# Turning a head pair's keys behind the next pair's scores in an RWKV-7 stage on one Trainium2 core

## The chip, the core and the metric

The program runs on one core of a Trainium2 chip. The core has five engines that each work through a queue of their own in order: TensorE (PE, with its weight loads shown apart as PEld), VectorE (DVE), ScalarE (ACT), GpSimd (POOL) and SyncE (SP, which only issues DMAs here). An engine waits for another through semaphores. The metric is the device time of one execution in microseconds, and the kernel before is given as the median of 3 runs. Beside it stands one profiled execution, from which every duration and every start below is taken. L12 is line 12 of the kernel before, except where the changed kernel is named.

## The reference

The trunk takes x of 1 x 512 x 1024 in float32. It has two layers, each a token mixer and a gated feed-forward block with a causal convolution, and a final RMSNorm. The mixer of the first layer is a chunked spatial gating MLP, that of the second the RWKV-7 time mixing, which the change touches:

```
r, k, v = xr @ w_r, xk @ w_k, xv @ w_v                     # xr, xk, ...: token-shifted mixes
w = -softplus(-(w0 + tanh(xw @ w1) @ w2)) - 0.5
a = sigmoid(a0 + (xa @ a1) @ a2);  g = sigmoid(xg @ g1) @ g2
kk = k * k_k, scaled to length 1 in each of 16 heads of 64
k = k * (1 + (a - 1) * k_a);  decay = exp(-exp(w))
for t in range(512):                                       # state S: 64 x 64 per head
    S = S * decay[t] + (S @ -kk[t]) (kk[t] * a[t])^T + v[t] k[t]^T
    y[t] = S @ r[t]
y = group_norm(y) * ln_w + ln_b + sum(r * k * r_k) * v
out = (y * g) @ w_o
```

The loop over tokens is computed in 8 chunks of 64 tokens. Within a chunk the products of keys and receptances form 64 x 64 triangular matrices (the scores), one of which must be inverted per head and chunk. From chunk to chunk only the state is handed on, by a product with "turned" keys: keys transposed and multiplied with the decay of the whole chunk.

## The kernel before

**Arithmetic.** A dense product in float32 is made of three matmuls on numbers split in a high and a low part (L320, L321, L322). Each has 128 rows and columns of the array and 512 columns of output. Other products are single matmuls on parts of the array: 64 rows x 128 columns for scores and turned keys, 64 x 64 in the scan, 32 x 32 in the inversion.

**Stages.** SGU mixer, feed-forward, RWKV-7 mixer, feed-forward, final norm. The mixer of RWKV-7 stands between about 573 and 850 us of the span. In it three streams of work are woven together by `weave`: a main one, a side one and a fill.

**The pairs (main).** Heads are worked through in 8 pairs p, one head on rows 0 to 63 of the array and one on rows 64 to 127. `pairs()` runs through them. For pair p it starts the decay steps of pair p + 2 (`decay`, matmuls L863, L865, L887, L895 into the "e" banks), makes the operands of pair p + 1 (`operands`: tiles ar and bk, two buffers each), and makes the products of pair p (`products`). These are:

- dg (L931, DVE): diagonal matrices of the chunk decays.
- Two halves of the scores, 4 chunks each. Each half is 16 matmuls (L938) of bk with ar, 8 for each head, one head into an "aux" bank and the other into a "us" bank. DVE evicts both with the masks into lq (L942), ACT copies a part into ti, the input of the inversion (L943), and three DMAs on SP's queue store lq into the DRAM scratch std (L946).
- Turned keys: 16 matmuls of bk with dg (L952), again 8 per head into "aux" and "us". ACT copies them into bt (L955) and SP stores bt into the DRAM scratch btd (L956).

A step of the decay of pair p + 2 follows each of the three. `done.add(p)` then marks the pair. `done` is what the stages below and the centering of values (`value`, L832, L838, and the bonus L847) go by.

**The inversion (side).** `invert(g)` inverts the triangles of four pairs at once: g = 0 for pairs 0 to 3, g = 1 for pairs 4 to 7. It copies ti, or a part of it, into a block tile (L1003 on DVE for g = 1), transposes it (L1006), runs 31 steps of two DVE instructions (L1014, L1015), transposes back (L1020 and the line behind it), and joins the blocks with two products of 32 x 32 matmuls (L1033, then L1036) through "aux" banks.

**The scan.** `scan(g)` goes through the 8 chunks of four pairs: products with the state (L1207, L1211), DVE's copy wt (L1210), the product with the inverse (L1220), the product with the turned keys that makes the next state (L1229), and the output (L1234). `load(g, c)` brings a chunk's operands back from DRAM on SP's queue: scores st (L1150), values vu (L1156), turned keys cbt (L1157). Chunk 0 of g = 0 is loaded earlier and into other tiles.

**The fill** is dense work: key and value projections, gates, and the output projection.

**What sets the order.** The stages are weaves one behind the other: the pairs until pair 3 is in `done`; then with inversion 0 beside them until pair 6 is; then `load(0, 0)`; then the rest of the pairs; then the pool of the pairs is closed and the pool of the scan takes its memory; then the scan of g = 0 with inversion 1 beside it; then the scan of g = 1. `weave` advances the side and the fill by rates per step of the main stream. `issue_after(x)` holds an instruction behind x on its engine. Within these bounds a scheduling layer fixes the order of each engine's queue when the program is built. PSUM is shared out by four tags, "mm", "aux", "e" and "us", with two banks each.

## Time and profile before

| | |
|---|---|
| median of 3 runs | 1267.81 us (1267.59 to 1269.96) |
| the profiled execution, its own time | 1264.91 us |
| its span, first to last instruction | 1263.1 us |
| mean granted clock of TensorE | 0.997 |
| PE, DVE, ACT busy in 600 to 640 us | 40.00, 32.11, 28.46 |
| in 720 to 760 us | 39.23, 37.35, 23.08 |
| in 760 to 800 us | 37.19, 29.25, 27.47 |
| in 800 to 850 us | 45.85, 35.88, 18.79 |

A row of the timeline gives start, duration, engine, line, operation, output and inputs, the rows and columns of the array for a matmul, shapes and a count. In square brackets stands how long the engine had been idle before it, and what ended that. Matmuls are pipelined, so their durations overlap, and what one costs is read from start to start. Rows of windows give a stretch of the span, its length, and each engine's busy time in it with the count of its instructions, then the granted clock, the share of DMA time and the rate in GB/s.

### The profile page before, as it was taken

The page shows a single profiled execution, that of the slowest core. Times are in us where ns is not written, and L with a number is a line of the kernel's source. Part 1 is how long each engine was busy: PE and PEld are TensorE (multiplying, and loading weights), DVE is VectorE, ACT ScalarE, POOL GpSimd, SP SyncE. Part 2 cuts the span into 40 slices and gives each one's busy share as a digit, 9 for nine tenths or more (in the row PEclk, how much of TensorE's full clock was granted, in tenths as well). Part 3 has the DMA queues.
Part 4 walks back from the last instruction along what each step waited for, and adds up shares of the span by engine and source line. Part 5 has one row for each costly group of instructions (what it writes and reads, how often), then busy time and mean ns, then how long its engine had stood idle before and what let it go on. Part 6 is the DMA issues. An engine that isn't in the chain of part 4 may idle for free.

```text
span 1263.1 us, 19531 instructions
## 1 busy us (share of the span) xinstructions
PE 1241.9 (98%) x7591; PEld 1007.9 (80%) x7591; DVE 856.1 (68%) x1403; ACT 629.7 (50%) x1082; POOL 98.0 (8%) x121
## 2 busy tenths in 40 slices
PE   9999999999999999999999999899999999999997
PEld 6878888888888888877777776678888888888886
DVE  6466568888886454675789897765677777773233
ACT  6544446556555433475676657423544544443322
POOL 4100200000000010000000022222000000000002
PEclk9999999999999999999999999999999999999998
DMA  7332357777656765325868799764222333333332
GB/s 258 104 100 84 130 167 240 247 252 245 195 166 203 228 215 184 97 91 192 218 200 226 215 244 230 213 171 138 96 95 91 99 100 100 96 88 105 92 92 80
DMA packets 115452, 201.65 MB, mean 160 GB/s; under 512 B 21600, under 2 KB 53600, under 8 KB 115360
## 3 DMA queue, kind: packets, MB, share of 16 engines
q10 hardware_dynamic: 39104, 112.87, 29.3%
q1 hardware_dynamic: 76256, 87.54, 23.2%
q8 instruction: 59, 0.97, 0.3%
q14 instruction: 33, 0.27, 0.1%
HBM read 152.93 MB, written 47.45 MB: 159 GB/s over the span
## 4 chain that ended last, share of the span: by engine, by line
PE 86%; DVE 6%; DMA 1%; issue 1%; ACT 1%; POOL 0%; SPq 0%; DVEq 0%; ACTq 0%; POOLq 0%
PE mm L320 9%; PE mm L322 9%; PE mm L321 9%; PE aux L320 6%; PE aux L322 6%; PE aux L321 6%; PE e L321 6%; PE e L320 6%; PE e L322 6%; PE us L321 5%; PE us L322 5%; PE us L320 5%; PE aux L938 1%; DVE tt L1015 1%; DVE pr L1014 1%; PE aux L952 1%
## 5 line engine op out<-in xcount | busy, mean ns | idle before, releaser
L236 ACT CAST w<-w 128x512 fp32r<-128x512 f32 x340 | 206.5, 611 | 360.8 <-PE e L322 91.1
L237 DVE TENSOR_TENSOR w<-w,w 128x512 fp32r<-128x512 f32 x340 | 232.1, 685 | 184.7 <-ACT w L236 184.4
L320 PE MATMUL mm<-mxh,w 128*128 128x512 f32 x416 | 169.7, 408 | 0.2 <-ACT vt L837 0.2
L321 PE MATMUL mm<-mxl,w 128*128 128x512 f32 x416 | 163.8, 394 | 0.0
L322 PE MATMUL mm<-mxh,w 128*128 128x512 f32 x416 | 163.7, 394 | 0.0
L347 POOL TENSOR_TENSOR ss<-ss,sq 128x512 f32<-128x512 f32 x30 | 40.7, 1355 | 770.7 <-issue 592.9
L320 PEld LDWEIGHTS mm<-mxh,w 128*128 128x128 f32 x416 | 78.1, 188 | 20.1 <-issue 3.3
L322 PEld LDWEIGHTS mm<-mxh,w 128*128 128x128 f32 x416 | 78.2, 188 | 16.7 <-issue 0.7
L321 PEld LDWEIGHTS mm<-mxl,w 128*128 128x128 f32 x416 | 78.2, 188 | 15.5 <-issue 1.3
L545 ACT ACTIVATE cv<-z,par 128x512 f32<-128x512 f32 x88 | 71.7, 817 | 29.4 <-DVE z L543 24.4
L322 PE MATMUL aux<-mxh,w 128*128 128x512 f32 x216 | 84.2, 390 | 0.3 <-DVE w L237 0.3
L320 PE MATMUL aux<-mxh,w 128*128 128x512 f32 x216 | 84.5, 391 | 0.0
L320 PE MATMUL us<-mxh,w 128*128 128x512 f32 x216 | 84.5, 391 | 0.0
L321 PE MATMUL aux<-mxl,w 128*128 128x512 f32 x216 | 84.1, 389 | 0.0
L321 PE MATMUL us<-mxl,w 128*128 128x512 f32 x216 | 84.1, 389 | 0.0
L322 PE MATMUL us<-mxh,w 128*128 128x512 f32 x216 | 84.0, 389 | 0.0
L320 PE MATMUL e<-mxh,w 128*128 128x512 f32 x208 | 81.4, 391 | 0.1
L321 PE MATMUL e<-mxl,w 128*128 128x512 f32 x208 | 81.1, 390 | 0.1
L322 PE MATMUL e<-mxh,w 128*128 128x512 f32 x208 | 80.9, 389 | 0.0
L546 DVE SCALAR_TENSOR_TENSOR cv<-z,par,cv 128x512 f32<-128x512 f32 x88 | 66.1, 752 | 19.9 <-ACT cv L545 19.9
L547 DVE SCALAR_TENSOR_TENSOR cv<-z,par,cv 128x512 f32<-128x512 f32 x88 | 66.0, 752 | 2.9
L322 PEld LDWEIGHTS aux<-mxh,w 128*128 128x128 f32 x216 | 40.5, 188 | 9.2 <-DVE w L237 0.8
(1089 smaller groups left out, 2574.8 us busy)
## 6 DMA issues: line engine op xcount, KB each, us to landing
w<-in_wup ACTq DMA_DIRECT2D x88, 512.0 KB, 3.6
w<-in_wdn ACTq DMA_DIRECT2D x32, 512.0 KB, 3.7
st<-std SPq DMA_DIRECT2D x30, 320.0 KB, 6.2
w<-wkd ACTq DMA_DIRECT2D x16, 512.0 KB, 4.9
w<-wvd ACTq DMA_DIRECT2D x16, 512.0 KB, 5.6
w<-wod ACTq DMA_DIRECT2D x16, 512.0 KB, 4.2
w<-in_wdn ACTq DMA_DIRECT2D x16, 384.0 KB, 3.4
w<-in_wsu ACTq DMA_DIRECT2D x8, 512.0 KB, 3.7
```

Of the source, the lines that this page charges most:

```text
L236: nc.scalar.copy(hi[r, :n], src)
L237: (lo_eng or nc.vector).tensor_tensor(lo[r, :n], src, hi[r, :n].bitcast(F32), ALU.subtract)
L320: mm(acc, wh, xh, start=first, stop=False)
L321: mm(acc, wh, xl, start=False, stop=False)
L322: mm(acc, wl, xh, start=False, stop=last)
L347: nc.gpsimd.tensor_tensor(self.ss, self.ss, self.sq, ALU.add)
L545: nc.scalar.activation(c, z[:, 2:], AF.Identity, scale=cw(2, i), bias=self.p("conv_b", l * 44 + i))
L546: nc.vector.scalar_tensor_tensor(c, z[:, 1:T + 1], cw(1, i), c, ALU.mult, ALU.add)
L547: nc.vector.scalar_tensor_tensor(c, z[:, 0:T], cw(0, i), c, ALU.mult, ALU.add)
L938: nc.tensor.matmul(qs[hd][:, c - ch.start, :], bk[H[hd], c, C * hd:C * hd + P], ar[H[hd], c, :], start=True, stop=True)
L952: nc.tensor.matmul(qs[hd][:, c, :], bk[H[hd], c, C * hd:C * hd + P], dg[H[hd], c, :], start=True, stop=True)
L1014: V.tensor_tensor(q, a, b, ALU.mult)
```

## The change

`products` is split in three. `scores(p, u, half)` makes one half of the scores; its first matmul is returned as `lead`, and the 15 others are held behind it. `diagonals(p, u)` makes dg. `turned(p, u, lead)` makes the turned keys, all 16 matmuls held behind `lead`, and now does `done.add(p)`. In `pairs()`, the first half of pair p's scores is followed by the turned keys of pair p - 1, which used to stand behind the second half of their own pair; dg is made between the two halves; the turned keys of pair 7 come behind the loop. The context manager `behind` is new, and the scan's `batch` uses it in place of its own three lines. The instructions are the same in kind and number.

```diff
+        @contextmanager
+        def behind(lead):
+            with ExitStack() as stack:
+                if lead is not None:
+                    stack.enter_context(tc.issue_after(lead))
+                yield
...
-        def products(p, u):
+        def scores(p, u, half):
...
-            dg = tile_([P, NCH, C], "dg", 1)
-            V.tensor_tensor(dg, self.c("id2", C).unsqueeze(1).to_broadcast([P, NCH, C]), bc(gc[:, p], C), ALU.mult)
             masks = self.c("masks", P)
-
-            for ch in (slice(0, U), slice(U, NCH)):
-                qs = [self.acc(tag).rearrange("p (c t) -> p c t", t=P) for tag in ("aux", "us")]
-                for c in range(ch.start, ch.stop):
-                    for hd in range(2):
+            ch = slice(U * half, U * half + U)
+            qs = [self.acc(tag).rearrange("p (c t) -> p c t", t=P) for tag in ("aux", "us")]
+            lead = None
+            for c in range(ch.start, ch.stop):
+                for hd in range(2):
+                    with behind(lead):
                         nc.tensor.matmul(qs[hd][:, c - ch.start, :], bk[H[hd], c, C * hd:C * hd + P], ar[H[hd], c, :],
                                          start=True, stop=True)
...
+                    lead = lead or self.last(mybir.EngineType.PE)
...
+            return lead
+
+        def diagonals(p, u):
+
+            u.dg = tile_([P, NCH, C], "dg", 1)
+            V.tensor_tensor(u.dg, self.c("id2", C).unsqueeze(1).to_broadcast([P, NCH, C]), bc(gc[:, p], C), ALU.mult)
+
+        def turned(p, u, lead=None):
+
             bt = tile_([P, NCH, 2, C], "bt", BT)
             qs = [self.acc(tag).rearrange("p (c t) -> p c t", t=C) for tag in ("aux", "us")]
-            for c in range(NCH):
-                for hd in range(2):
-                    nc.tensor.matmul(qs[hd][:, c, :], bk[H[hd], c, C * hd:C * hd + P], dg[H[hd], c, :],
-                                     start=True, stop=True)
+            with behind(lead):
+                for c in range(NCH):
+                    for hd in range(2):
+                        nc.tensor.matmul(qs[hd][:, c, :], u.bk[H[hd], c, C * hd:C * hd + P], u.dg[H[hd], c, :],
+                                         start=True, stop=True)
             for hd in range(2):
                 S.copy(bt[:, :, hd, :], qs[hd])
             nc.sync.dma_start(btd[:, :, p].rearrange("c p a t -> p c (a t)"), bt.rearrange("p c a t -> p c (a t)"))
-            yield
+            done.add(p)
...
-                for _ in products(p, units[p]):
-                    next(nxt, None)
-                    yield
-                done.add(p)
+                lead = scores(p, units[p], 0)
+                if p:
+                    turned(p - 1, units[p - 1], lead)
+                next(nxt, None)
+                yield
+                diagonals(p, units[p])
+                scores(p, units[p], 1)
+                next(nxt, None)
+                yield
+                next(nxt, None)
+                yield
+            turned(p, units[p])
+            yield
```

In the changed kernel the scores stand at L943, their evictions at L948 and L949, their stores at L952, dg at L958, the turned keys at L967 and their store at L971. The inversion's products are L1057 and L1060, the decay's matmuls L870, L872, L894 and L902, the bonus L854, the transposition L1030.

**First place: the last scores of pair 0 and the first of pair 1, on PE.** In the names, bk_4984 holds the keys of the earlier pair and bk_5090 those of the later one. Before, the turned keys stood by themselves between dense matmuls:

```order
L320 MATMUL mm_5072<-mxh_4838,w_794_5018 128x512
L321 MATMUL mm_5072<-mxl_4839,w_794_5018 128x512
L887 MATMUL e_5170<-cst,sq_5162 128x2 x4
L322 MATMUL mm_5072<-mxh_4838,w_794_5018 128x512
L952 MATMUL aux_5187<-dg_5098,bk_4984 128x64
L952 MATMUL us_5188<-dg_5098,bk_4984 128x64
...
L320 MATMUL mm_5217<-mxh_4759,w_803_5073 128x512
...
L322 MATMUL mm_5217<-mxh_4786,w_803_5073 128x512
L938 MATMUL aux_5251<-ar_5085,bk_5090 128x128
L938 MATMUL us_5252<-ar_5085,bk_5090 128x128
...
L863 MATMUL e_5269<-lr_4357,l_785_4998 128x512
```

In the changed kernel they follow the later pair's scores directly:

```order
L322 MATMUL mm_5195<-mxh_4786,w_803_5073 128x512
L943 MATMUL aux_5227<-ar_5085,bk_5090 128x128
L943 MATMUL us_5228<-ar_5085,bk_5090 128x128
...
L967 MATMUL aux_5246<-dg_5141,bk_4984 128x64
L967 MATMUL us_5247<-dg_5141,bk_4984 128x64
...
L870 MATMUL e_5267<-lr_4357,l_785_4998 128x512
L870 MATMUL e_5268<-lr_4358,l_786_4999 128x512
```

One stretch of 64-row matmuls stands where two were, and the turned keys have moved past a dozen dense matmuls.

**Second place: the start of the first inversion, on DVE.** In the names, sq_5808 and sq_5806 are decay tiles, li is the transposed block. Before:

```order
L942 TENSOR_TENSOR lq_5848<-us_5839,cst 128x4x128
L875 SCALAR_TENSOR_TENSOR sq_5808<-cst,sq_5808 128x512
L931 TENSOR_TENSOR dg_5971<-cst,gc 128x512
L1006 STREAM_TRANSPOSE li_5828<-ix_5827 128x32x32
L1014 TENSOR_TENSOR pr_5830<-li_5828,tt_5829 128x31
```

In the changed kernel:

```order
L948 TENSOR_TENSOR lq_5848<-aux_5838,cst 128x4x128
L948 TENSOR_TENSOR lq_5848<-us_5839,cst 128x4x128
L882 SCALAR_TENSOR_TENSOR sq_5806<-cst,sq_5806 128x512
L1030 STREAM_TRANSPOSE li_5826<-ix_5825 128x32x32
L948 TENSOR_TENSOR lq_5959<-aux_5949,cst 128x4x128
```

No dg stands ahead of the transposition any more, and the eviction of the next pair's first scores stands directly behind it.

**Third place: the end of the pairs, on PE.** Here bk_6171 (before) and bk_6149 (changed) hold the keys of pair 7, ix and li are the inversion's transposed blocks. Before:

```order
L1033 MATMUL aux_6310<-ix_6305,ti_4860 32x32 x16
L938 MATMUL aux_6360<-ar_6166,bk_6171 128x128 x4
L1033 MATMUL aux_6310<-ix_6305,ti_4860 32x32 x16
...
L938 MATMUL us_6453<-ar_6166,bk_6171 128x128 x3
L938 MATMUL aux_6452<-ar_6166,bk_6171 128x128 x4
...
L1036 MATMUL aux_6489<-li_6306,tt_6309 32x32 x16
L322 MATMUL mm_6508<-mxh_5501,w_1047_6331 128x512
...
L952 MATMUL us_6521<-dg_6358,bk_6171 128x64 x4
L952 MATMUL aux_6520<-dg_6358,bk_6171 128x64 x5
...
L1036 MATMUL aux_6489<-li_6306,tt_6309 32x32 x16
L832 MATMUL mm_6577<-cst,v_6506 128x128 x2
L1036 MATMUL aux_6559<-li_6306,tt_6309 32x32 x16
```

In the changed kernel:

```order
L1057 MATMUL aux_6395<-ix_6283,ti_4860 32x32 x16
L322 MATMUL mm_6508<-mxh_5537,w_1044_6309 128x512
L967 MATMUL us_6573<-dg_6450,bk_6149 128x64
L1060 MATMUL aux_6489<-li_6284,tt_6287 32x32 x32
L1060 MATMUL aux_6537<-li_6284,tt_6287 32x32 x16
L967 MATMUL us_6573<-dg_6450,bk_6149 128x64 x7
L1060 MATMUL aux_6537<-li_6284,tt_6287 32x32 x16
L320 MATMUL mm_6508<-mxh_5550,w_1045_6311 128x512
L321 MATMUL mm_6508<-mxl_5551,w_1045_6311 128x512
L967 MATMUL aux_6572<-dg_6450,bk_6149 128x64 x8
L322 MATMUL mm_6508<-mxh_5550,w_1045_6311 128x512
```

The turned keys of pair 7 stood ahead of three quarters of the inversion's second product (L1036); now half of them stand behind all of it (L1060), and the two heads' rows stand apart. On SP's queue the store of these keys is still the last of the pairs and still stands ahead of the loads of the scan's chunk 1.

More of the change, by code (lines that the diff above doesn't have):

```diff
@@ L2 @@
 import math
-from contextlib import ExitStack
+from contextlib import ExitStack, contextmanager
 import numpy as np
@@ L938, in products @@
                         nc.tensor.matmul(qs[hd][:, c - ch.start, :], bk[H[hd], c, C * hd:C * hd + P], ar[H[hd], c, :],
                                          start=True, stop=True)
-                lq = tile_([P, U, 2, P], "lq", 2)
-                for hd in range(2):
-                    V.tensor_tensor(lq[:, :, 1 - hd], qs[hd], masks.unsqueeze(1).to_broadcast([P, U, P]), ALU.mult)
-                    S.copy(ti[g][H[hd], i, ch], lq[H[hd], :, 1 - hd, 0:C])
-                f = lq.rearrange("p c a t -> p c (a t)")
@@ L945, in products @@
-                for hd, o, n, q in ((0, P, P, 0), (0, 2 * P, C, P + C), (1, 0, P + C, C)):
-                    nc.sync.dma_start(std[g][ch, H[hd], i, o:o + n].rearrange("c p t -> p c t"), f[H[hd], :, q:q + n])
-                yield
+                    lead = lead or self.last(mybir.EngineType.PE)
+            lq = tile_([P, U, 2, P], "lq", 2)
+            for hd in range(2):
+                V.tensor_tensor(lq[:, :, 1 - hd], qs[hd], masks.unsqueeze(1).to_broadcast([P, U, P]), ALU.mult)
+                S.copy(ti[g][H[hd], i, ch], lq[H[hd], :, 1 - hd, 0:C])
@@ new lines, in scores @@
+            f = lq.rearrange("p c a t -> p c (a t)")
+            for hd, o, n, q in ((0, P, P, 0), (0, 2 * P, C, P + C), (1, 0, P + C, C)):
+                nc.sync.dma_start(std[g][ch, H[hd], i, o:o + n].rearrange("c p t -> p c t"), f[H[hd], :, q:q + n])
+            return lead
[3 more added lines that the diff above has]
+        def turned(p, u, lead=None):
@@ L1178, in batch @@
                 for n, (i, hd) in enumerate(ih):
-                    with ExitStack() as behind:
-                        if lead is not None:
-                            behind.enter_context(tc.issue_after(lead))
+                    with behind(lead):
                         one(i, hd, n)
```

3 lines of the change are left out of this document (1 added, 2 removed).

## The prediction

> **What bounds the kernel now.** I read the page first, then the windows over the stage that the change touches, then the timelines of PE, DVE and SP there. Line numbers are those of the kernel before.
>
> ```profile
> span 1263.1 us, 19531 instructions
> PE 1241.9 (98%) x7591; PEld 1007.9 (80%) x7591; DVE 856.1 (68%) x1403; ACT 629.7 (50%) x1082; POOL 98.0 (8%) x121
> PE 86%; DVE 6%; DMA 1%; issue 1%; ACT 1%; POOL 0%; SPq 0%; DVEq 0%; ACTq 0%; POOLq 0%
> ```
>
> Over the whole span TensorE (PE) is the bound. The second row says 98% busy, and the third, the chain of waits, gives it 86%. But the average hides the stage in question. The windows (stretch, its length, then busy time and count of PE, PEld, DVE, ACT, POOL) show two bounds there:
>
> ```profile
> 640.00:680.00 40.00, 40.00 (x298) 30.05 (x297) 35.79 (x70) 30.59 (x57) 0.23 (x2) 1.00 0.76 216
> 680.00:700.00 20.00, 19.86 (x162) 16.23 (x162) 19.67 (x44) 11.83 (x25) 0.61 (x2) 1.00 0.79 231
> 730.00:740.00 10.00, 9.23 (x108) 7.03 (x108) 9.52 (x23) 5.17 (x10) 1.64 (x3) 1.00 1.02 273
> 740.00:750.00 10.00, 10.00 (x135) 7.10 (x133) 9.60 (x21) 5.96 (x14) 2.56 (x6) 1.00 1.08 270
> 750.00:760.00 10.00, 10.00 (x128) 8.08 (x128) 9.56 (x28) 4.13 (x10) 3.27 (x3) 1.00 1.06 238
> 780.00:790.00 10.00, 7.99 (x186) 6.25 (x186) 5.00 (x11) 6.91 (x13) 4.39 (x6) 1.00 0.81 209
> ```
>
> Up to 680 PE has no idle time and VectorE (DVE) has some, so PE time saved there is time saved. From 680 to 700, and from 730 to 760, DVE is as full as PE, because it carries the two inversions (L1014, L1015). There, PE time saved may only become waiting. From 780 to 790 PE stands idle for 2.0 us.
>
> **What a change of array shape costs.** This is the price that the change is about: a batch of 64-row matmuls between dense ones (PE timeline: start, duration, line, rows*columns of the array).
>
> ```profile
> 602.58 0.39 PE L321 MATMUL mm<-mxl,w 128*128 128x512 f32 x1
> 602.81 0.39 PE L322 MATMUL mm<-mxh,w 128*128 128x512 f32 x1
> 603.13 0.37 PE L938 MATMUL aux<-ar,bk 64*128 64x128 f32 x1
> 603.14 0.37 PE L938 MATMUL us<-ar,bk 64*128 64x128 f32 x1
> 603.34 0.27 PE L938 MATMUL aux<-ar,bk 64*128 64x128 f32 x1
> ...
> 603.46 0.27 PE L938 MATMUL aux<-ar,bk 64*128 64x128 f32 x1
> ...
> 604.01 0.27 PE L938 MATMUL aux<-ar,bk 64*128 64x128 f32 x1
> ...
> 604.22 0.50 PE L320 MATMUL mm<-mxh,w 128*128 128x512 f32 x1
> 604.56 0.39 PE L321 MATMUL mm<-mxl,w 128*128 128x512 f32 x1
> ...
> 712.95 1.16 PE L938 MATMUL aux<-ar,bk 64*128 64x128 f32 x8
> 714.03 0.69 PE L1033 MATMUL aux<-ix,ti 32*32 32x32 f32 x32
> ```
>
> From start to start, dense matmuls take 0.23, and a pair of 64-row passes, one on each half of the rows, takes 0.11 or 0.12. Going in, the first start comes after 0.32 and the second pair after 0.20. Coming out, the first dense start comes after 0.21 and the next after 0.34. So each of the four steps is about 0.10 longer than its kind: 0.39 for a visit, 0.195 for each change. The last two rows price passes without a partner: 8 on one half take 1.08, less the 0.2 of the changes still 0.108 each, so a pass that finds no partner costs what a pair costs.
>
> By the Trainium skill (TensorEngine Tiling (Array Packing), section Tiling Modes, Key Properties), changing the tiling mode drains TensorE, and changing the tile alone does not. If a drain meant the full 0.27 of the pass in flight, 19 changes would be worth 5.1 us instead of 3.7; the rows spread the price over both sides of the change, and they decide.
>
> **The change part by part: PE's own sum.** The PE order differs between the first batch of pair 1 and a place in the middle of chunk 7 of the scan. It holds the same 1309 matmuls in both kernels. Counting the places in it where the array shape changes gives 94 before and 78 now up to the first scan matmul, and 60 against 57 behind it. That is 19 fewer, at 0.195: 3.7 us less. Pairing gets slightly worse at the end of the pairs, where "us" and "aux" rows now stand in rows of six to eight: counted pair by pair, 284 slots of two passes' time against 280, so 4 x 0.108 = 0.4 more. PE's own work is **3.3 us shorter**. Computation, evictions and DMAs are the same in number. The new wait of bk's writes (two buffers, and the old one is now read half a pair longer) I cost at nothing: up to pair 4 it has some 8 us until the next scores; with that cover gone it is two 0.6 us writes and a 0.6 us copy.
>
> **What DVE gives back at the first inversion.** DVE's and PE's rows there:
>
> ```profile
> 663.98 0.69 DVE L942 TENSOR_TENSOR lq<-aux,cst 128x512 f32<-128x512 f32 x1 [0.50 <-PE us L938]
> 667.54 0.69 DVE L931 TENSOR_TENSOR dg<-cst,gc 128x512 f32<-128x512 f32 x1 [1.15 <-PE us L952]
> 668.15 2.24 DVE L1006 STREAM_TRANSPOSE li<-ix 128x1024 f32<-128x1024 f32 x1
> 675.18 0.69 DVE L942 TENSOR_TENSOR lq<-aux,cst 128x512 f32<-128x512 f32 x1 [0.15 <-PE us L938]
> 710.26 2.01 DVE L1020 STREAM_TRANSPOSE ix<-tt 128x1024 f32<-128x1024 f32 x1
> 712.32 0.69 PE L1033 MATMUL aux<-ix,ti 32*32 32x32 f32 x32 [0.53 <-DVE ix L1020]
> ```
>
> DVE works through 42.1 us from L1006 to L1020 with 0.15 of waiting on scores, and PE then waits 0.53 for it. By the order now and the prices above, PE stands 1.4 earlier by L942 of pair 4 and 1.9 earlier at L1033. DVE's L1006 stands ahead of that dg, so it starts at about 668.15 - 1.15 - 0.6 - 1.4 = 665.0. But its list up to L1020 is 0.7 longer (one L849 more, one dg less and a little else), and it waits 0.8 to 2 for the next scores. That puts L1033 0.6 to 1.7 earlier; I take **1.1**. The other 0.8 turns into a longer wait.
>
> **What the late last turn gives back.** Behind L1033 the new order packs more ahead of what the scan needs.
>
> ```profile
> 717.92 0.60 PE L938 MATMUL us<-ar,bk 64*128 64x128 f32 x3
> 721.61 0.68 DVE L1003 COPY ix<-ti 32x1024 f32<-32x1024 f32 x1 [0.78 <-ACT ti L943]
> 725.17 0.69 PE L1036 MATMUL aux<-li,tt 32*32 32x32 f32 x32
> 725.81 0.59 ACT L955 COPY bt<-us 128x512 f32<-128x512 f32 x1
> 726.42 0.36 SPq L956 DMA_DIRECT2D btd<-bt  x1
> SPq L1150 <- DMA btd<-bt: 1.3, 1, 1.3
> btd<-bt SPq DMA_DIRECT2D x1, 512.0 KB, 4.8
> 731.33 1.13 SPq L1150 DMA_DIRECT2D st<-std  x2
> 732.50 1.24 SPq L1156 DMA_DIRECT2D vu<-vtd  x2
> vu<-vtd SPq DMA_DIRECT2D x2, 64.0 KB, 4.9
> 740.43 0.69 PE L1207 MATMUL us<-vu,st 128*64 128x64 f32 x16
> 774.56 0.43 DVE L1210 COPY wt<-us 128x256 f32<-128x256 f32 x1
> ```
>
> Pair 7's turned keys end at 725.17, 12.85 after L1033. ACT copies them, SP stores them at 726.42, and the first load of the scan's chunk 1 (L1150) waits until that store has landed, since its buffer lies where the pairs' buffers lay. Its vu lands near 733.1 + 4.9 = 738.0, 2.4 before PE wants it at 740.43. Now pair 7 turns behind all of its scores, after three of the inversion's four second products. In the new order, from L1033 to the last turned row: 128 small products 5.0 (0.62 per 16), 16 scores 1.7, 16 turned rows partly paired 2.8, 16 alone 3.5, three centering rows 0.7, 8 dense 1.8, 14 changes 2.7, together 18.2. The same prices give 0.5 too much for the stretch before, so I take 17.7, 4.8 longer. With the 1.1 gained it ends 3.7 later, so does the store, and vu lands at 741.7: chunk 1 starts **1.3 later** than now. From there to where the orders meet again PE has 2.9 less to do (52.6 against 55.5 by the same prices). By this route the end moves by -1.6.
>
> DVE's route is tighter. Pair 7's last scores start 2.4 later behind L1033, are paired (1.1 instead of 1.5) and gain the 1.1: 0.9 later, and with them L1003, from which DVE is full until L1210 of chunk 5 at 774.56. Its work up to there is the same in both orders, and it idles 0.9 in it now, so that L1210 comes 0 to 0.9 later. PE then has 0.75 less to do to the meeting point: -0.75 to +0.15, less whatever of the 2.0 idle between 780 and 790 does not come again.
>
> **The sum.** Of the 3.3 I count **0.4** as reaching the end, between the two routes and nearer to the DVE one, since DVE is the fuller engine there. On the profiled execution's own time (span 1263.1, 1264.91 with what lies around it) that is 1264.5. This execution lies 2.9 below the median of the runs shown, 1267.81, so against the median I forecast **1267.4**.
>
> **Rivals.**
> 1. PE's counts stand whole: DVE waits for PE less than I think, and the idle 2.0 of 780 to 790 takes up the rest. For it: PE is 98% busy. Against it: DVE at 95% and more from 680 to 770. Gain 3.3, so 1264.5. Chance 0.2.
> 2. Slower: the late store of pair 7. It decides once the store lands later than 731.2 + 2.4 + 2.9 = 736.5, when the stall of chunk 1 passes what PE has less to do. The "aux" half of the last turn needs a bank that ACT must first empty of the inversion's product; should that add 3 to 4 to the 3.7, chunk 1 comes 4.3 to 5.3 later, DVE's steps queued behind its wt copy (the second inversion) come later with it, and 1.4 to 2.4 is left, with DVE's 0.9 up to 3.3. I price it at +3.0, 1270.8. For it: loads at a DMA share above 1.0 from 730 to 760. Against it: ACT is half idle there. Chance 0.2.
> 3. The edit merges less than it says: only the turns of pairs 0, 1 and 2 stand wholly behind scores in the new order. If only these count, it is 3 x 0.39 - 0.4 = 0.8 of gain before anything is given back; the time is 1267.0 to 1267.8, inside the forecast's band.
>
> **How the numbers follow.** About 0.2% (2.5 us) is what a measurement of this kernel can tell from no change. The forecast with rival 3 has 0.6 and lies within it; rival 1 is faster by more (0.2), rival 2 slower by more (0.2). The bounds of the unknown waits are -3.3 and +3.0: 1264.5 to 1270.8.
>
> **What would show it.** Right: fewer entries into 64-row batches before 680, and PE a good microsecond earlier at pair 4; a longer wait than 0.53 at the first L1033; the last btd store issued near 730; PE waiting at chunk 1's first scan matmul. The two traces should run in step from chunk 8 on. Wrong: L1033 earlier by the whole 1.9 (then DVE was no bound); a store near 727 (then the late turn costs nothing, rival 1); a store after 732 and a stall above 2 us at chunk 1 (rival 2); or a clock below 1.00 in the windows.

## The result, and the profile after

| | us | against before |
|---|---|---|
| kernel before, 4 runs | 1268.88 (1267.59 to 1270.29) | |
| changed kernel, 4 runs | 1281.63 (1279.85 to 1285.44) | 1.0104 (95%: 1.0077 to 1.0131) |
| changed kernel, 4 more runs on another occasion | 1278.84 (1278.15 to 1282.20), before 1268.09 | 1.0083 (1.0062 to 1.0104) |
| forecast | 1267.4, range 1264.5 to 1270.8 | no change |

The change costs 11 to 13 us. It was forecast to cost nothing. The profiled execution took 1285.44. One run of all that follow, 1384.69 us at a clock of 0.845 (the profiled one of the ten with scores held together), was of a second, slower kind and is left out.

The page of the changed kernel, where it answers to the rows shown of before:

```profile
span 1283.6 us, 19532 instructions
PE 1252.8 (98%) x7591; PEld 1019.0 (79%) x7591; DVE 857.7 (67%) x1403; ACT 630.4 (49%) x1082; POOL 97.3 (8%) x121
PEclk9999999999999999999999898999999999999998
PE 84%; DVE 6%; DMA 2%; ACT 1%; issue 1%; POOL 1%; DVEq 0%; SPq 0%; ACTq 0%; POOLq 0%
```

PE is as busy as before by its share, and the chain of waits looks alike. The row that differs is PEclk, the granted clock of TensorE, which falls in the middle of the RWKV stage. In the page of before it stands at 9 up to the last slice:

```profile
PEclk9999999999999999999999999999999999999998
```

The windows of the changed kernel show where (stretch, its length, busy time and count of PE, PEld, DVE, ACT, POOL, then the granted clock, DMA share, rate). The edges are those of the clock's own steps in the trace:

```profile
669.09:672.50 3.41, 3.41 (x50) 3.33 (x46) 3.41 (x8) 2.35 (x6) 0.00 (x0) 1.00 0.85 204
672.50:675.92 3.42, 3.42 (x24) 2.97 (x24) 2.25 (x7) 0.00 (x0) 0.12 (x1) 0.50 0.89 272
710.05:713.46 3.41, 1.18 (x3) 0.68 (x4) 0.89 (x5) 1.48 (x5) 0.00 (x0) 1.00 0.38 116
713.46:716.88 3.42, 3.42 (x9) 2.65 (x8) 3.32 (x6) 1.70 (x3) 0.00 (x0) 0.50 0.56 149
727.12:730.53 3.41, 3.41 (x136) 3.02 (x130) 3.00 (x5) 3.13 (x8) 0.00 (x0) 1.00 0.64 121
730.53:744.18 13.65, 13.65 (x74) 10.80 (x72) 7.35 (x16) 3.83 (x7) 1.24 (x2) 0.50 0.36 102
791.97:795.38 3.41, 1.42 (x49) 1.13 (x48) 2.83 (x8) 2.95 (x4) 0.00 (x0) 1.00 1.06 267
795.38:802.21 6.83, 6.65 (x82) 5.32 (x84) 2.80 (x5) 6.24 (x11) 1.85 (x4) 0.50 0.70 177
```

Four times the clock is 0.50, for 1, 1, 4 and 2 windows of 3.41 us: 27.3 us in all. Every such stretch begins right behind a window of 3.41 us that held something unusual. In two of them PE stood idle for most of it (1.18 and 1.42 of 3.41 busy). In the other two PE was busy throughout: at 669 with scores, turned keys and the decay's 2-column matmuls, at 727 with 32x32 products and turned keys without a partner. In the trace of before the clock is 1.00 through the whole stage. Of the 20.5 us between the two profiled executions, half clock in the stage accounts for up to 13.7 (half of 27.3), and 0.8 is lost ahead of the stage. What the rest is made of is taken up with the experiments.

PE's rows behind 727 show what the longest of them is made of:

```profile
728.00 0.43 PE L967 MATMUL us<-dg,bk 64*128 64x64 f32 x2
728.36 1.71 PE L1060 MATMUL aux<-li,tt 32*32 32x32 f32 x96
730.00 2.79 PE L967 MATMUL us<-dg,bk 64*128 64x64 f32 x14
...
734.86 3.67 PE L967 MATMUL aux<-dg,bk 64*128 64x64 f32 x16
```

The last pair's turned keys run first on one half of the rows ("us"), then on the other ("aux"), never both at once, and at half clock a pass takes 0.20 to 0.23 instead of 0.108.

### The profile page after: what moved, and what is told of

Its sections match the earlier page's. It is cut to its first block, busy times and chain, and to the rows that moved or that the text cites. A ratio compares the mean times of both kernels' runs of the same rounds, so it can differ in the third digit from the quotient of the medians.

```text
span 1283.6 us, 19532 instructions
## 1 busy us (share of the span) xinstructions
PE 1252.8 (98%) x7591; PEld 1019.0 (79%) x7591; DVE 857.7 (67%) x1403; ACT 630.4 (49%) x1082; POOL 97.3 (8%) x121
## 4 chain that ended last, share of the span: by engine, by line
PE 84%; DVE 6%; DMA 2%; ACT 1%; issue 1%; POOL 1%; DVEq 0%; SPq 0%; ACTq 0%; POOLq 0%
PE mm L320 9%; PE mm L322 8%; PE mm L321 8%; PE aux L320 6%; PE aux L322 6%; PE aux L321 6%; PE e L321 6%; PE e L320 6%; PE e L322 6%; PE us L321 5%; PE us L322 5%; PE us L320 5%; PE aux L967 1%; PE aux L943 1%; DMA w<-g1d 1%; PE e L902 1%
## 5 line engine op out<-in xcount | busy, mean ns | idle before, releaser
L320 PE MATMUL mm<-mxh,w 128*128 128x512 f32 x416 | 172.8, 415 | 0.5 <-DVE rt L856 0.4
L322 PE MATMUL mm<-mxh,w 128*128 128x512 f32 x416 | 166.0, 399 | 0.0
L322 PEld LDWEIGHTS mm<-mxh,w 128*128 128x128 f32 x416 | 79.3, 191 | 17.7 <-issue 0.8
```

What stands on the lines that cost most here:

```text
L320: mm(acc, wh, xh, start=first, stop=False)
L322: mm(acc, wl, xh, start=False, stop=last)
```

## The experiments

Two theories were set against each other. **Gate**: TensorE's clock is halved behind a window of little array work, whether or not PE idles, and the change makes such windows by packing small work together. **Stall**: later stores and copies make PE wait, and the clock follows from its idling. For each timed run its ratio to before has a 95% interval; "clock" is the mean granted clock over its runs. Over 58 runs of before, on three occasions, the clock is 0.9943, that is 14 us at half clock in a mean run (28 more on a fourth occasion have 0.9934). In the trace of before 7.6 us are the last ones of its span, from 1255.5 on. Over the 8 runs of the changed kernel it is 33 us. In the same 58 runs, a run that has lost 1 us more to the clock (time times what the clock lacks to 1) is 0.9 us longer.

**The changed kernel again**, unaltered, on another occasion.

> The changed kernel itself, unaltered, beside the two variants of this call. Gate (its loss is half clock behind lean stretches, wherever the free-running windows fall): 1278 to 1285 again with a clock of 0.984 to 0.989. If the loss had been one chip's or one hour's, it would come out at 1270 or less.

Measured: 1278.84, 1.0083, clock 0.988. The loss is the change's own.

**Each part alone.** First the scores of a half held together, and the turned keys where they were:

```diff
-                if p:
-                    turned(p - 1, units[p - 1], lead)
...
+                turned(p, units[p])
```

> Only the scores of a half are held together; the turned keys stay behind their own pair's second half, as in the kernel before. Two theories of the 12.7 us that the change cost. Gate: the trace of the changed kernel shows the granted clock at one half for 3.4, 3.4, 13.7 and 6.8 us between 672 and 802 us, each beginning right behind 3.4 us in which TensorE did little but turned keys, 32x32 products or nothing; so the loss comes from packing turned keys with other small work. Stall: the loss comes from stores and copies that come later on SP and ACT (TensorE waits 2.8 us for a copy of vt at 710), and the clock falls only because TensorE stood idle. Here neither is moved: both expect the time of before, 1266 to 1270, and a mean clock of 0.994 to 0.998.

Measured: ratio 1.0003 (0.9985 to 1.0021), 1269.5. Holding scores together costs nothing and gains nothing by itself. Then the move for pairs 0 to 2 only, and for pairs 3 to 7 only:

```diff
-                if p:
+                if p and late(p - 1):      # late(q): q < 3 in the one, q >= 3 in the other
                     turned(p - 1, units[p - 1], lead)
...
+                if not late(p):
+                    turned(p, units[p])
```

> The turned keys of pairs 0, 1 and 2 alone go behind the next pair's scores; pairs 3 to 7 turn behind their own. Both theories: these three batches (3.9 us each without a dense matmul in the changed kernel's trace) tripped nothing there, so the clock stays at 0.994 to 0.998, and the time is that of before less up to 1.2 us (3 x 0.39): 1265.5 to 1269. If the time rises by more than 5 us with a lower clock, the early merges are at fault too.

> The complement: pairs 0 to 2 turn behind their own scores, pairs 3 to 7 behind the next pair's, pair 7 behind the loop. Both theories put the loss here: 1278 to 1284 and a mean clock of 0.983 to 0.990. If it is below 1274, the loss needs early and late merges together.

Measured: 1273.69, 1.0044 (1.0027 to 1.0061), clock 0.993, for the early pairs; 1277.69, 1.0074 (1.0059 to 1.0089), clock 0.990, for the late ones. The first is a miss of both theories: three early batches were to save about 1 us and cost 5.7. In its trace the clock is full in the stage up to 716; it is halved for 3.4 us at 716 and 6.8 at 784. And though the edit does not name pair 7, its turned keys (728.38 to 730.3) stand behind three quarters of the inversion's second product there, against one quarter in before, and their store goes out at 731.57 instead of 726.42. (The edit also puts pairs 3 to 7 into `done` one step sooner than before; whether that moved them was not tested.) What this is worth is worked out below. The late part makes most of the loss, with the same 13.65 us at half clock as the whole change:

```profile
726.25:739.90 13.65, 13.65 (x75) 11.11 (x74) 7.17 (x17) 3.78 (x7) 1.03 (x2) 0.50 0.34 100
```

**More work for TensorE.** Dense matmuls into the banks that the turned keys then overwrite, ahead of the turned keys of pairs 3 to 7, and in the second run more of them, and into the inversion's banks too:

```diff
             with behind(lead):
+                for hd in range(2):
+                    for _ in range(1 if p >= 3 else 0):      # second run: 2
+                        nc.tensor.matmul(qs[hd].rearrange("p c t -> p (c t)"), r.lr[0][:, 0:P], r.lr[0], start=True, stop=True)
                 for c in range(NCH):
```

> The changed kernel with two dense 128x512 matmuls more ahead of the turned keys of each of pairs 3 to 7, into banks that the turned keys then overwrite: TensorE has 2 x 0.23 us and two shape changes of 0.195 more to do five times, 4.3 us in all, and the lean windows hold 0.43 us more of full-array work. Gate: the window that tripped at 672.5 and the one at 730.5 no longer trip; the clock rises to 0.990 or more and the time falls in spite of the added work, to 1272 to 1279. Stall: the added work only delays what is late already: 1284 to 1288, clock not higher than 0.988.

> As the run with added dense matmuls, but more of them: four ahead of the turned keys of each of pairs 3 to 7, and one into each of the four banks of inversion 0's products, all overwritten afterwards. That is 24 x 0.23 + 9 x 0.39 = 9 us of TensorE work more than in the changed kernel, and no stretch of small work under a third of full work is left before 760 us. Gate: the clock comes up to 0.993 or more, the time to 1272 to 1279 in spite of the work. Stall: 1288 or more.

Measured: 1275.08, 1.0064 (1.0040 to 1.0088), clock 0.991: with 4.3 us more to do it is 4 to 6 us faster than the changed kernel by the medians, though its ratio's interval overlaps that kernel's. In its trace the stretches at 672 and 730 are gone; two others are there (685 and 747), behind windows in which PE idled 1.0 and 2.2 us. That speaks for the gate and against the stall. The second run does not: 1288.81, 1.0159 (1.0121 to 1.0196), clock 0.987, in the stall's range. Its windows and rows say why:

```profile
709.54:712.95 3.41, 1.81 (x48) 1.47 (x44) 3.34 (x4) 0.00 (x0) 0.00 (x0) 1.00 0.72 197
712.95:730.01 17.06, 17.06 (x112) 13.06 (x112) 3.10 (x5) 7.11 (x10) 1.12 (x2) 0.50 0.26 70
```

```profile
711.92 0.69 PE L1062 MATMUL aux<-ix,ti 32*32 32x32 f32 x32 [1.59 <-DVE ix L1047]
714.11 3.25 PE L970 MATMUL us<-dg,bk 64*128 64x64 f32 x14
718.44 3.03 PE L970 MATMUL aux<-dg,bk 64*128 64x64 f32 x13
```

PE waits 1.59 for DVE there, the clock falls, and 14 and 13 passes follow without a partner, at half clock, for five windows. So this run has more lean time, not less, and does not separate the theories. Its forecast by the gate was wrong by 10 us.

**The gate by itself.** The kernel before, with TensorE work alone put behind its end:

> The kernel before with TensorE work alone put behind its end, to measure the clock gate by itself. Between warm stretches of 32 full-array 128x512 matmuls stand: 90 pairs of turned-key matmuls (64 rows, 64 columns streamed); 90 pairs of score matmuls (64 rows, 128 columns); 250 pairs of 32x32 products; 90 turned-key matmuls on one half of the rows only; then turned keys and full matmuls mixed, 12 pairs to 1, 10 to 2 and 7 to 3, seven times each. TensorE never waits in any of them. Gate (the clock is halved behind 3.4 us of little array work, without any idle time): the 32x32 products and the lone turned keys run at half clock from the second window on, the paired turned keys probably, the scores and the mixes with 2 and 3 full matmuls not. Stall (only idle time trips it): the clock stays at 1.00 in all of them.

The windows of the four plain kinds, in that order:

```profile
1285.00:1304.00 19.00, 19.00 (x345) 19.00 (x344) 0.00 (x0) 0.00 (x0) 0.00 (x0) 1.00 0.01 3
1333.00:1352.00 19.00, 19.00 (x344) 19.00 (x342) 0.00 (x0) 0.00 (x0) 0.00 (x0) 1.00 0.01 3
1388.00:1405.00 17.00, 15.84 (x580) 15.70 (x582) 0.00 (x0) 0.00 (x0) 0.00 (x0) 0.50 0.02 5
1443.00:1469.00 26.00, 26.00 (x124) 26.00 (x124) 0.00 (x0) 0.00 (x0) 0.00 (x0) 0.50 0.00 1
```

Paired turned keys and scores run at full clock; for the paired turned keys half clock had been thought probable. 32x32 products and turned keys without a partner run at half clock, though nothing else is there to wait for and PE is 26.00 of 26.00 busy in the last row. The three mixtures of pairs with full matmuls ran at full clock. Stall has fallen as the only cause.

From the traces I then worked out a **row use**: for each window of 3.41 us the time in which columns stream, times the share of the 128 rows in use. A full fp32 matmul of 512 columns counts as 1 (16 passes take 6.85 in the second fence below, 0.43 each). A turned-key pass has an eighth of its columns and half its rows: 0.026 of the 0.108 that it takes. That is 0.245 alone and 0.49 in a pair. A 32x32 pass, a sixteenth of the columns on a quarter of the rows, counts 0.007, of some 0.022. Over the traces of before, the change and twelve of the variants, between 30 and 1250 us, all but at most one of the 25 to 28 windows under 0.375 were followed by half clock, and 2 to 4 of the nearly 100 between 0.375 and 0.52. The two windows in which PE never idled had 0.37 (669) and 0.35 (727). The ends of records are modelled, so the row use is an estimate, and the counts depend a little on where a pass is taken to stream. Two more runs measured it by mixtures.

> As the first gate measurement, with mixtures: lone turned keys (one half of the rows) 12, 10 and 7 to 1, 2 and 3 full-array fp32 128x512 matmuls, then 32, 26 and 20 pairs of 32x32 products to 1, 2 and 3 of them, seven times each; each period is about 3.4 us and TensorE never waits. Gate: with 1 full matmul (0.45 us, 13% of a window) both kinds still trip, with 3 (40%) neither does; where it turns lies the bound. Stall: none trips.

With one full matmul to 12 lone turned keys the clock went to half at 1301, for seven windows; with 2 and 3 it stayed at 1.00. The 32x32 products stayed at 1.00 in all three mixtures, so half of the expectation for one full matmul fell. A full matmul there is two passes, some 0.86 us and not the 0.45 of the expectation, so this mixture lies near the bound: in three windows, from 1288 to 1298, it has a row use of 0.40, at full clock, and only the window that ends at 1301 has less, 0.31 to 0.36 by where its last pass is put. With two full matmuls it is 0.40 or more; for the 32x32 mixtures the count of overlapping small passes is too rough to say.

> As the two gate measurements, with one shape of work only, so that no change of shape and no waiting comes in: turned keys in pairs and alone, 4 pairs to 12 lone ones, 8 to 8, 10 to 6, 12 to 4 and 14 to 2, eight times each (about 28 us a kind). A pair in 0.216 us uses 0.49 of what dense matmuls use, a lone one 0.245, so the five kinds use 0.31, 0.37, 0.40, 0.43 and 0.46. Gate with the bound near 0.4 that the traces give: the first two run at half clock in part, the last two at full clock, the middle one may do either. If lone rows as such trip it, whatever their share, the third and the fourth do too.

```profile
1298.00:1338.00 40.00, 40.00 (x237) 40.00 (x237) 0.00 (x0) 0.00 (x0) 0.00 (x0) 0.50 0.00 0
1376.00:1418.00 42.00, 42.00 (x295) 42.00 (x294) 0.00 (x0) 0.00 (x0) 0.00 (x0) 0.50 0.00 1
1450.00:1477.00 27.00, 27.00 (x401) 27.00 (x398) 0.00 (x0) 0.00 (x0) 0.00 (x0) 1.00 0.01 2
1506.00:1534.00 28.00, 28.00 (x445) 28.00 (x444) 0.00 (x0) 0.00 (x0) 0.00 (x0) 1.00 0.01 2
1563.00:1590.00 27.00, 27.00 (x463) 27.00 (x460) 0.00 (x0) 0.00 (x0) 0.00 (x0) 1.00 0.01 2
```

```profile
1284.44 6.85 PE L635 MATMUL aux<-cst 128*128 128x512 f32 x16
1291.92 2.73 PE L635 MATMUL aux<-cst 64*128 64x64 f32 x23
```

As forecast: the mixtures worth 0.31 and 0.37 fall to half clock, those worth 0.40, 0.43 and 0.46 do not. By the windows' own count the last one that tripped had 0.366 and the leanest that did not 0.383. With passes of one shape it is the share of the rows in use that decides here, and lone rows as such do no harm.

**What in the change makes lean windows.** Nothing held behind the first matmul of a batch; pair 7's keys turned one step sooner; both:

```diff
-                    lead = lead or self.last(mybir.EngineType.PE)
```
```diff
                 next(nxt, None)
                 yield
+                if p == KT - 1:
+                    turned(p, units[p])
...
-            turned(p, units[p])
-            yield
```

> The changed kernel without the holding: the turned keys go where the change puts them, but no matmul is held behind the first of its batch. In its order the lean stretch of the inversion's second product and the last turned keys (5.0 and 3.4 us without a dense matmul in the changed kernel) is broken up by dense matmuls; the one at pair 4 stays, and the stores are as late as in the changed kernel. Gate: the 13.7 us at half clock around 730 to 744 go, 1272 to 1277 with a clock of 0.990 to 0.993. Stall: as the changed kernel, 1280 to 1284.

> The changed kernel with pair 7's keys turned one step sooner, before the last yield of the pairs. The last store then is issued sooner, but a stretch of 5.1 us of small work without a dense matmul stands in the order there still. Gate: as the changed kernel, 1278 to 1284 and a clock of 0.985 to 0.989. Stall (the late store of pair 7 is what costs): 1272 to 1277.

> Nothing is held behind the first matmul of a batch, and pair 7's keys are turned one step sooner; the turned keys of the other pairs stay behind the next pair's scores, as in the change. The two single edits had cut the loss by 9.3 us (nothing held) and by 6.5 us (sooner). Gate and the late store as two separate causes: together they leave the saving of TensorE's own work, 1264 to 1269 with a clock of 0.993 to 0.996, at or below the kernel before. If they are one cause: as nothing held alone, 1271 to 1275.

| | us | ratio | clock |
|---|---|---|---|
| nothing held | 1272.32 | 1.0040 (1.0022 to 1.0058) | 0.994 |
| held, pair 7 sooner | 1275.13 | 1.0053 (1.0037 to 1.0070) | 0.987 |
| nothing held, pair 7 sooner | 1273.11 | 1.0036 (1.0019 to 1.0054) | 0.990 |

The first is the gate's forecast, and its clock is that of before. The stretch that is at half clock in the changed kernel is at full clock here:

```profile
720.00:745.00 25.00, 23.13 (x358) 18.58 (x358) 21.70 (x47) 15.71 (x31) 2.93 (x6) 1.00 0.73 191
```

So holding the batches together at the turned keys' new place, not the place alone, halves the clock there: 6.5 to 9 us of the loss (1278.8 and 1281.6 against 1272.3). But 4.7 us to before remain at the same clock. The second run fits the stall's range: the same low clock as the changed kernel, and yet 4 to 6 us less. That points to a second cause, the late last turn, which is in the first run too. SP's and PE's rows of the run with nothing held:

```profile
730.04 0.36 SPq L970 DMA_DIRECT2D btd<-bt  x1
735.80 1.14 SPq L1173 DMA_DIRECT2D st<-std  x2
736.98 1.24 SPq L1179 DMA_DIRECT2D vu<-vtd  x2
...
vu<-vtd SPq DMA_DIRECT2D x2, 64.0 KB, 6.7
...
744.17 0.69 PE L1228 MATMUL us<-vu,st 128*64 128x64 f32 x16 [0.51 <-DMA vu<-vtd]
```

The last store goes out at 730.04 (726.42 in before), the first load behind it at 735.80 (731.33), the values land 6.7 after their issue instead of 4.9, and chunk 1 starts at 744.17 instead of 740.43. The third run was expected to remove both causes and came out in the range that was given for one cause: with pair 7's keys turned sooner and nothing held, their lone passes stand beside the inversion's last products, and the clock is halved there again, for 6.83 us:

```profile
725.29:728.70 3.41, 3.41 (x76) 3.10 (x76) 3.24 (x5) 2.68 (x5) 0.00 (x0) 1.00 0.68 190
728.70:735.53 6.83, 6.83 (x33) 6.04 (x33) 6.14 (x19) 3.12 (x7) 0.00 (x0) 0.50 0.26 80
```

**The two causes told apart.** The traces of these runs allow it, as an estimate. The first column is the time from the start of the inversion's first product (L1033 in before) to the last store. The second is without half of the time at half clock in it. The third is what the median is above that of before when 0.9 us are taken off for each us that the runs lose more to the clock.

| | to the last store | without the clock | time over before, without the clock |
|---|---|---|---|
| before | 14.1 | 14.1 | |
| changed kernel | 21.3 | 17.0 | 3.4 |
| the same again | 21.2 | 17.8 | 4.3 |
| nothing held | 17.6 | 17.6 | 4.1 |
| pairs 0 to 2 only | 19.4 | 17.7 | 3.9 |
| pairs 3 to 7 only | 22.2 | 17.7 | 3.6 |
| held, pair 7 sooner | 16.2 | 14.2 | -0.8 |
| nothing held, pair 7 sooner | 17.0 | 14.7 | 0.3 |

Where the last store comes some 3 us later, about 4 us remain when the clock is taken off; in the two runs where it does not, nothing remains. So the clock and the late last turn look like two causes, of 6 to 9 and about 4 us in the changed kernel, and the third run took the late turn away but not the half clock. The early pairs' 5.7 are the same two, 1.8 of clock and 3.9. The other variants fit less sharply: 18.8 in the second column and 2.3 in the third with one dense matmul a bank, 15.2 and 2.5 with the banks e and us below. Why 3 us of store are worth 4 is not shown.

**Partners for the last rows.** One word, in the changed kernel:

```diff
-            qs = [self.acc(tag).rearrange("p (c t) -> p c t", t=C) for tag in ("aux", "us")]
+            qs = [self.acc(tag).rearrange("p (c t) -> p c t", t=C) for tag in (("e", "us") if p >= 6 else ("aux", "us"))]
```

> The changed kernel with one word changed: the turned keys of pairs 6 and 7 go into banks of the tags e and us instead of aux and us. The aux banks hold the inversion's products there, which is why the two heads' rows stand apart in the changed kernel's order, each pass without a partner on the other half of the rows. Now 4 passes of turned keys stand alone in the order instead of 28. Gate, as the records have shown it so far (the clock is halved behind 3.41 us in which rows times time are used less than about 0.4 of what dense matmuls use): the lean places near 727 to 738 shrink, the half clock there goes from three or four windows to one or two; 1271 to 1276 and a clock of 0.990 to 0.993. If pairing is beside the point and only the late place of the last turn counts: 1278 to 1283, as the changed kernel.

Measured: 1275.21, 1.0045 (1.0031 to 1.0059), clock 0.990: 4 to 6 us faster than the changed kernel, with the turn at the same place of the program. Its store goes out at 730.64 instead of 739.18. The passes now alternate between the halves, and the half clock there lasts two windows:

```profile
728.28 0.27 PE L967 MATMUL us<-dg,bk 64*128 64x64 f32 x1
728.28 0.27 PE L967 MATMUL e<-dg,bk 64*128 64x64 f32 x1
```
```profile
729.32:736.14 6.82, 6.82 (x49) 4.83 (x46) 5.10 (x13) 2.63 (x5) 1.23 (x2) 0.50 0.56 152
```

**The saving without the harm.** Pairs 0 to 2 turn in one batch with their own second half of scores, so no store comes later. Pairs 3 to 7 are not held, but by this edit they too turn in the step of their second half of scores, one step sooner than in the kernel before (the expectation says as before). Then the banks as well; and, for comparison, the banks with scores held together alone:

```diff
+                diagonals(p, units[p])
+                scores(p, units[p], 0)
...
+                lead = scores(p, units[p], 1)
+                turned(p, units[p], lead if p < 3 else None)
```

> Scores of a half held together, and pairs 0 to 2 turn directly behind the second half of their own scores in one batch (no delay of half a pair); pairs 3 to 7 turn as in the kernel before. It saves the shape changes of three visits (1.2 us) without moving any store later. Gate: its lean stretches of 3.1 us at pairs 0 to 2 hold 28% of full-array work, more than what tripped; clock 0.992 to 0.997, time 1265 to 1269. If merges by themselves upset the order of all that follows, as the run with early merges did: 1271 to 1275.

> The run with scores held together and pairs 0 to 2 turned in one batch with their own second half, with the turned keys of pairs 6 and 7 in the banks e and us as well. By its order the places under the bound cover 1.6 windows' worth of starting points, the kernel before 2.2 and the changed one 4.3, by the same count. Gate: clock 0.994 to 0.997, time 1263 to 1267, below the kernel before. If the banks only shift work into others' way: 1267 to 1271.

> Only the scores of a half held together, the turned keys at their old place, and those of pairs 6 and 7 in the banks e and us. By its order 1.6 windows' worth under the bound. Gate: clock 0.994 to 0.997, time 1265 to 1268. Against the run before it tells what the early batches of pairs 0 to 2 bring beside the gate (1.2 us by the price of a shape change).

| | us | before beside it | ratio | clock |
|---|---|---|---|---|
| own batch, pairs 0 to 2 | 1266.90 | 1268.09 | 0.9991 (0.9973 to 1.0008) | 0.994 |
| the same, with banks e and us | **1264.49** | 1268.51 | **0.9964** (0.9950 to 0.9978) | 0.994 |
| scores together, banks e and us | 1267.62 | 1268.51 | 0.9987 (0.9974 to 1.0001) | 0.994 |

The second is faster than the kernel before by 4.0 us, and so than the changed one. Its clock is that of before beside it (0.993), not higher as forecast, so it does not gain by the clock. Against the third it has two things more: the early batches, worth 1.2 by the price of three visits, and the sooner turn of pairs 3 to 7. Its last store goes out 11.4 behind the inversion's first product, against 12.5 in the third and 14.1 in before:

```profile
721.71 0.37 SPq L971 DMA_DIRECT2D btd<-bt  x1
```

How the 3 us between them divide was not tested.

## Why the prediction was wrong

(One correction first: where the words ahead of the prediction and the prediction speak of 16 matmuls, for a half of the scores they count passes, of which the trace shows two per matmul of the program. A half is 8 matmuls and 16 passes, so that `lead` holds 7 others, and a pair's turned keys are 16 and 32.)

**The step that failed is one that the sum does not have.** Every duration in it is at the clock of before, read as 1.00 in the windows of the stage. "A clock below 1.00 in the windows" stood last among the things that would show it wrong, with no mechanism, price or chance. The change makes lean windows, and with them some 18 us more at half clock in a mean run than before (33 against 14), up to 9 us of time. The trace of before had the warning: its windows hold 0.40 and 0.36 to 0.39 of row use at 723 and at 784, near the bound. By an estimate from the traces, the places from which 3.41 us fall under the bound cover about 1 window's worth of starting points there, and 3 to 5 in the changed kernel's. The page's clock of 0.997 said nothing, because that execution met none of them. Another execution of the same instructions did, in the run with the five mixtures, which holds the whole kernel before ahead of them:

```profile
726.70:736.94 10.24, 10.24 (x87) 7.75 (x86) 6.86 (x20) 5.02 (x11) 1.24 (x2) 0.50 0.68 177
788.13:798.37 10.24, 10.24 (x153) 8.16 (x151) 4.53 (x10) 4.94 (x9) 3.26 (x3) 0.50 0.50 137
```

In the first two gate runs the same instructions met 3.4 us of it, at 684 in the one and at 789 in the other. So where a stretch falls under the bound differs from run to run, and a run's luck is part of its time. The profiled execution's being 2.9 us under the median, which the prediction noted and did not ask about, was the trace of it: the runs of before range from a clock of 0.990 to 0.997, and each lost microsecond of clock goes with 0.9 us of time.

By the Trainium skill (TensorE: Matmul & The Clock Gate, Part 1), the clock has the two states half and full, and a free-running window of 3.41 us decides. The steps of 3.42, 6.83 and 13.65 us at 0.50 agree. It puts the fall down to an idle window; here PE was busy for the whole of the windows at 669 and 727 and in the lone rows behind the end, and the measurement decides: busy is not enough.

**PE's own sum, 3.3 shorter.** The price of 0.195 for a change of shape was not refuted, but the changed kernel kept little of it. Pair 4's second scores were to be evicted 1.4 earlier:

```profile
664.24 0.69 DVE L948 TENSOR_TENSOR lq<-aux,cst 128x512 f32<-128x512 f32 x1 [0.45 <-PE us L943]
...
PE e L894 <- ACT sq L884: 0.4, 1, 0.4
PE e L902 <- DVE n L897: 0.2, 1, 0.2
```

They are at 664.24 against 663.98. All of this execution's stage stands 0.8 later from the start (3.4 us at half clock at 20 us), so 0.5 was gained; 0.6 went into two waits of the decay's matmuls that before does not have. The sum had no new wait at the early merges; that was wrong, in small. That the early merges alone cost 5.7 us in a run of their own goes by the clock and the last store, as told above.

**L1033 1.1 earlier.** It came 5.6 later (717.90 against 712.32), behind the half clock at 672 and 713 and behind a wait that was not on the list: the bonus matmul L854 waits 2.8 for ACT's copy of vt, which waits for the store of the vt before it.

**The late last turn.** The place was right, the size was not, and the rival that held it (chance 0.2, 1270.8) was nearer than the forecast. Its reason, the bank that the "aux" half must wait for, fits the run with other banks, in which the two halves alternate. In the run without the gate's share the store is issued at 730.04, where the forecast had "near 730", 3.6 later; that is in part luck, for the inversion's first product comes 0.1 later there instead of 1.1 earlier, and the way from it to the store is 3.5 longer instead of 4.8. The term that was mis-sized is what follows: chunk 1 was to start 1.3 later and starts 3.7 later, since the store lands after 5.6 instead of 4.8 and the values after 6.7 instead of 4.9. That run is 4.7 us slower than before, so by that run and the table above the change would have been about 4 us slower even without a fallen clock, outside the range. In the changed kernel itself half clock comes on top:

```profile
739.18 0.36 SPq L971 DMA_DIRECT2D btd<-bt  x1
742.64 1.13 SPq L1174 DMA_DIRECT2D st<-std  x2
...
753.07 0.69 PE L1229 MATMUL us<-vu,st 128*64 128x64 f32 x16
```

The store goes out 9 us later than forecast, and chunk 1 starts 12.6 after before.

**DVE as the bound.** DVE is busy 10.24 of 20.00 us between 720 and 740 in the changed kernel, 18.18 in before: it waits for a slow PE. The term cannot be judged there.

```profile
720.00:740.00 20.00, 20.00 (x319) 17.48 (x319) 10.24 (x20) 12.81 (x23) 0.04 (x1) 0.76 0.43 109
```

**Right:** the traces run in step from chunk 8 on, 19.7 to 20.3 apart to the end of the stage; more passes without a partner at the end of the pairs, though the 0.4 us that they were priced at is their least part: they halve the row use.

## What to carry to other kernels

Count what a reordering does to the leanest window of about 3.4 us, not only to the sum: here rows times time under some 0.38 of full use halved the clock for at least one window more, even with PE busy all along. Look, too, at when the last store goes out that the next stage waits for: 3 us there were worth 4 here. Small matmuls belong between dense ones, or two to a slot on both halves of the rows; a batch that is held together is safe only if what stands beside it is not small too. And the spread of the runs is a reading: if the profiled execution lies well under the median, look at each run's clock before pricing a change at full clock.

## What the runs showed that was not expected

The clock is halved with PE 100% busy, and the bound lies between 0.366 and 0.383 of row use in steady mixtures of one shape. A 64-row pass alone and a pair of them take the same 0.108 us, so a lone one halves the row use without showing in any busy time. Once down, the clock came back after one window only where the row use at half clock was high: behind 713 one window of dense work was enough, from 730 it took four, with lone turned keys in the first three. And a reordering of a pair's work moved the time of the whole by 11 to 13 us, 6 to 9 of them through windows that hold 3.4 us each, while its counted sum of work got smaller.
